# Where the tiles lie in memory, and the order of an opening: a hybrid decoder block on one core

## The chip, the cores and the metric

The kernel runs on one core of a Trainium2 chip. The metric is the device time of one execution in microseconds (us). Three runs of the kernel before took 1753.73, 1755.06 and 1755.92 us; the median, 1755.06, is what the change is compared with.

The engines have short names in the profile. PE is TensorE, which multiplies matrices; PEld is its load of the stationary operand; DVE is VectorE; ACT is ScalarE; POOL is GpSimd; SP issues most DMAs. SBUF is the on-chip memory of 128 partitions. Every tile has an address, the same in each partition, given here in KiB from the low end.

## The reference

x has 256 rows (tokens) and 2048 columns, all in float32. One layer is computed: a SwiGLU feed-forward network (FFN) at half weight, a mixer, and a second FFN.

```python
for l in range(DEPTH):                      # DEPTH = 1
    x = x + 0.5 * swiglu_ffn(rms_norm(x, ffn1_norm[l]), ffn1_w_gate[l], ffn1_w_up[l], ffn1_w_down[l])
    z = rms_norm(x, mix_norm[l]) @ w_in[l]              # 2048 -> 5120, five parts of 1024
    ...                                                 # conv + RG-LRU * gelu, and a gated short conv
    y = jnp.concatenate([rms_norm(y_lru, lru_out_norm[l]), rms_norm(y_sc, sc_out_norm[l])], axis=-1)
    x = x + y @ w_out[l]
    x = x + 0.5 * swiglu_ffn(rms_norm(x, ffn2_norm[l]), ffn2_w_gate[l], ffn2_w_up[l], ffn2_w_down[l])
return rms_norm(x, final_norm)

def rms_norm(x, gain):
    return x * rsqrt(mean(x * x, axis=-1) + 1e-6) * gain

def swiglu_ffn(x, w_gate, w_up, w_down):                # 2048 -> 5632 -> 2048
    return (silu(x @ w_gate) * (x @ w_up)) @ w_down
```

## The kernel before, in words

**Weights in two parts.** A float32 operand is split into a rounded part `hi` and a rest `lo`, and a product is built from hi x hi, lo x hi and hi x lo. Weights come in units of 4 x 128 rows by 512 columns, 1 MB each. `load` (L155) issues a unit's DMA into a raw tile; `parts_of` (L169) makes `hi` by a copy on ScalarE and `lo` by a subtraction on VectorE. TensorE streams `hi` and `lo` as the moving operand, 512 columns wide, and holds a 128 x 128 piece of the activations as the stationary one (`multiply`, L194). One unit is 24 matmuls when it meets both row blocks of x, 12 when it meets one. In the mixer (`columns`) the roles are the other way round.

**Pools and their places.** Pools are declared in this order and lie one above another in that order, from the low end: `const` (with `xres`, the 256 x 2048 x of 16 KiB, to 22 KiB), `raws` (3 raw tiles of 8 KiB, to 46), `splits` (two `hi` from 46 to 62, two `lo` from 62 to 78), `bigs` (ten tiles of 8 KiB for activations in two parts, 78 to 158), `work` (to 163). On top stands the pool of the FFN that is running, `fp` (L406): 13 tiles `keep` of 2 KiB (163 to 189), one more `hi` and one more `lo` (189 to 205), and two raw tiles tagged `kept` (205 to 221). While an FFN runs, every third unit that is split takes the `hi` and `lo` of that pool (L171 to L174); the others take turns at the two of `splits`. In the mixer there is no such pool, and two pools of the mixer's own stand in its place.

**An FFN.** The first 512 columns of gate and up are computed as usual, in eight units named g and u (`ps_g`, `ps_u`). The remaining 5120 columns go in five steps of 1024. Each step treats two row blocks of x by two column blocks of the weight as a 2 x 2 product, done with seven multiplications instead of eight (`seven`, L344). Its operands are sums of blocks: weight sums are made by VectorE in the raw tiles, and the sums of x's blocks once by `seven_of` (L314), whose first call makes `spare` and splits it and whose second part, `rest`, makes three more sums and splits them. In the first FFN these are tiles named `xs`; for the down projection the same is done with the hidden activations in the `keep` tiles, named `hs`. Units named `_p` belong to the seven products (12 matmuls), units named `_x` to the rest of the inner dimension (24).

**The opening of the first FFN.** x is in transposed form only after TensorE's transposes (`Norm.turn`, L220, with four column blocks of 128 per call). The row factor of the norm, 1/sqrt(mean of squares), is not known at first: the first eight units use x times the gain without it, and the factor is put on their results. For the later blocks, `plain` joins x's two parts in float32 (`v`), `normalise` multiplies `v` by the row factor spread over the columns (`norm.bc`, made by `rows` with two small matmuls) and splits it again, and `sums` calls `seven_of`. The squares are sums along rows by ScalarE (`squares`, L213), one instruction for each of four column blocks and two row blocks; `factor` adds them and calls `inv_sqrt` (L257), whose square root is on ScalarE, with a table load ahead of it.

**What sets the order.** Each engine works through its instructions in one order. As long as `Engine.pinned` is true, calls through `pe`, `act` and `dve` stay in program order; that holds from the first unit to the end of the second up unit (L522). Elsewhere a planner may pull an instruction ahead when its operands are ready. DMA issues on SP aren't pinned. The dictionary `follow` (L477) names what is called behind each unit of the opening, and `meanwhile` (L600) what is called within a block: at the first step, `sums` again (which then is `rest`) and `normalise(3)`.

Of the kernel before, what the change touches and what calls it, by code (L numbers as in the profile page):

```python
# [10 lines left out]
F32 = mybir.dt.float32  # L11
F32R = mybir.dt.float32r
AF = mybir.ActivationFunctionType
# [3 lines left out]
P = 128  # L17
D = 2048
# [30 lines left out]
def hybrid_block(ctx: ExitStack, tc: tile.TileContext, a: dict, out: bass.AP):  # L49
# [22 lines left out]
            owed[0] -= cost  # L72

    const = ctx.enter_context(tc.tile_pool(name="const", bufs=1))
    raws = ctx.enter_context(tc.tile_pool(name="raws", bufs=3))
    splits = ctx.enter_context(tc.tile_pool(name="splits", bufs=2))
    bigs = ctx.enter_context(tc.tile_pool(name="bigs", bufs=10))
    work = ctx.enter_context(tc.tile_pool(name="work", bufs=2))
    psum = ctx.enter_context(tc.tile_pool(name="psum", bufs=8, space=bass.MemoryType.PSUM))

    def bank(name):
# [3 lines left out]
        return ap.bitcast(F32)  # L85


    xres = const.tile([P, NT, D], F32, name="xres")

    def load_x(c):  # L90
        cs = slice(c * CW, (c + 1) * CW)
        nc.sync.dma_start(xres[:, :, cs], x[:, cs].rearrange("(t p) d -> p t d", p=P))
# [53 lines left out]
    def big(name):  # L146

        return bigs.tile([P, UK, 2 * S], F32R, tag="big", name=name)
# [6 lines left out]
    def load(src, name, pieces=((0, UK),), loaded=None, kept=False):  # L155
        if kept is None and extra and not turn_of["hold"]:
            turn_of["raw"] += 1
            kept = turn_of["raw"] % 5 > 2
        if kept:
            raw = extra[0].tile([P, UK, CW], F32, tag="kept", name=f"raw_{name}", bufs=2)  # L160
        else:
            raw = raws.tile([P, UK, CW], F32, tag="raw", name=f"raw_{name}")
        for i, e in pieces:
            nc.sync.dma_start(raw[:, i:e, :], src[i * P : e * P].rearrange("(j p) c -> p j c", p=P))
            if loaded:
                loaded(i)
        return raw
# [39 lines left out]
    class Norm:  # L207
# [2 lines left out]
            self.xT = [None] * (KD // UK)  # L210
            self.ss = work.tile([P, NT, NC_D], F32, tag="ss", name=f"ss_{name}")

        def squares(self, c):  # L213
            for t in range(NT):
                junk = work.tile([P, CW], F32, tag="junk", name=f"junk_{self.name}_{c}_{t}", bufs=1)
                act.activation(
                    junk, xres[:, t, c * CW : (c + 1) * CW], AF.Square, accum_out=self.ss[:, t, c : c + 1]
                )

        def turn(self, ks, plain=None):  # L220

# [35 lines left out]
    def inv_sqrt(tot, n, name, w=NT):  # L257
        def t(tag):
            return work.tile([P, w], F32, tag=f"{tag}{w}", name=f"{tag}_{name}")

        v, s, y, q, r = (t(tag) for tag in "vsyqr")
        dve.tensor_scalar(v, tot, 1.0 / n, EPS, op0=ALU.mult, op1=ALU.add)
        act.activation(s, v, AF.Sqrt)
        dve.reciprocal(y, s)
        dve.tensor_tensor(q, y, y, op=ALU.mult)
        dve.tensor_tensor(q, q, v, op=ALU.mult)
        dve.tensor_scalar(q, q, -0.5, 1.5, op0=ALU.mult, op1=ALU.add)
        dve.tensor_tensor(r, y, q, op=ALU.mult)
        return r


# [131 lines left out]
        done(0, 0, d, [s1])  # L403

    def ffn(tag, norm, after, opening=False):
        with tc.tile_pool(name=f"ffn{tag}", bufs=1) as fp:  # L406
            extra.append(fp)
            turn_of["hold"] = True
            wg, wu, wd = (a[f"ffn{tag}_w_{s}"][0] for s in ("gate", "up", "down"))

# [30 lines left out]
            def room(u):  # L441
                for t in range(NT):
                    vs[t, u] = quad(keep(f"v{tag}_{u}_{t}"))
                return {t: vs[t, u] for t in range(NT)}

            def plain(u):

                x = f32(norm.xT[u])
                for t, v in room(u).items():
                    dve.tensor_tensor(  # L450
                        v, x[:, :, t * P : (t + 1) * P], x[:, :, S + t * P : S + (t + 1) * P], op=ALU.add
                    )
# [22 lines left out]

            if opening:
                follow = {  # L477
                    (0, "u"): [lambda: plain(0)],
                    (1, "u"): [flush, lambda: plain(1)],
                    (2, "g"): [norm.rows, lambda: normalise(0)],  # L480
                    (2, "u"): [lambda: normalise(1), sums],
                    (3, "g"): [lambda: normalise(2)],
                }
            else:
                follow = {
                    (0, "g"): [flush],
                    (0, "u"): [norm.factor, lambda: plain(0)],
                    (1, "g"): [norm.rows, lambda: plain(1), lambda: normalise(0)],
                    (1, "u"): [lambda: normalise(1), sums, lambda: plain(2)],
                    (2, "g"): [lambda: normalise(2), lambda: plain(3)],  # L490
                }
            ps = {(m, t): bank(f"ps_{m}{tag}_0_{t}") for m in "gu" for t in range(NT)}
            Engine.pinned = opening
            for u in range(KD // UK):
                for m, w in (("g", wg), ("u", wu)):
                    n = f"{m}{tag}_0_{u}"
                    src = w[u * UK * P : (u + 1) * UK * P, :CW]
                    if opening and (u, m) == (0, "g"):
                        pieces = ((0, 1), (1, 2), (2, 4))
                        raw = load(src, n, pieces, lambda i: load_x(1) if i == 1 else None)  # L500
                        blk = parts_of(raw, n, pieces, lambda i: norm.turn((i,) if i < 2 else (2, 3)))
                        for j in range(UK):
                            for t in range(NT):
                                yh, yl = stationary(norm.xT[u], t)[j]
                                pe.matmul(ps[m, t], yh, blk[j][0], start=j == 0, stop=False)
                                pe.matmul(ps[m, t], yl, blk[j][0], start=False, stop=False)
                                pe.matmul(ps[m, t], yh, blk[j][1], start=False, stop=False)
                        continue
                    raw = load(src, n)
                    if opening and u < 2 and m == "u":  # L510
                        load_x(u + 2)
                    blk = parts_of(raw, n, ((0, 2), (2, 4)), (lambda i: None) if opening else None)
                    if opening and u < 3 and m == ("u" if u < 2 else "g"):
                        if u == 2:
                            norm.squares(3)
                            norm.factor()
                        norm.turn(range(4 * u + 4, 4 * u + 8), room(u + 1) if u else None)
                        for c in ((0, 1), (2,), ())[u]:
                            norm.squares(c)
                    multiply([(ps[m, t], stationary(norm.xT[u], t), u == 0, u == 3) for t in range(NT)], blk)  # L520
                    pump(1.5)
                    if (u, m) == (1, "u"):  # L522
                        Engine.pinned = False
                    for fn in follow.get((u, m), ()):
                        fn()
            units.append(big(f"x{tag}_3"))
            xs = list(enumerate(units))[2:]
            for t in range(NT):
                sg = keep(f"sg{tag}_0_{t}")
# [47 lines left out]
            for s in range(5):  # L577
                cs = (CW + 2 * s * CW, 2 * CW + 2 * s * CW)
                sg = {}

                def total(ps, tiles):
                    for p in tiles[1:]:
                        dve.tensor_tensor(tiles[0], tiles[0], p, op=ALU.add)
                    if not tiles:
                        return ps
                    dve.tensor_tensor(tiles[0], ps, tiles[0], op=ALU.add)
                    return tiles[0]

                def gate(t, n, ps, tiles):
                    g = total(ps, tiles)  # L590
                    sg[t, n] = tiles[0] if tiles else keep(f"z{tag}_{s}")
                    act.activation(sg[t, n], g, AF.Silu)

                def up(t, n, ps, tiles):
                    dve.tensor_tensor(sg[t, n], total(ps, tiles), sg[t, n], op=ALU.mult)
                    if (t, n) == (1, 0):
                        settle()
                    waiting.append((1 + 2 * s + n, t, sg[t, n], s % 2 == 0))

                def meanwhile(i):  # L600
                    if i == 1:
                        settle()
                    elif s == 0:
                        (sums, lambda: normalise(3))[i // 2]()

                seven(wg, (0, 1), cs, sf, xs, f"g{tag}_{s}", keep, gate, meanwhile)
                seven(wu, (0, 1), cs, sf, xs, f"u{tag}_{s}", keep, up)
                if s % 2 == 0:
                    down(s == 4)
# [341 lines left out]
```

## Time and profile before

| What | Value |
|---|---|
| Median of three runs | 1755.06 us |
| Lowest and highest run | 1753.73 and 1755.92 us |
| Span of the profiled execution, from its first to its last instruction | 1753.8 us |
| Busy: PE, DVE, ACT | 1734.0, 1490.1, 1049.6 us |
| Mean granted clock of TensorE | 0.997 |
| DMA, mean over the span | 196 GB/s |

The page gives the span of the profiled execution and no other time of it; the span lies 1.3 us under the median. A page's line of an engine gives its busy time, the share of the span and the number of instructions. In the timeline, a row merges instructions of one kind that follow one another; its first number is the start in us, the second the time from the start of the first to the end of the last. Tile names are without their numbers. L42 is the helper through which all calls of the three engines go, so rows are told apart by tiles.

### The profile page before, as it was taken

What the parts mean: (1) busy time and instruction counts of PE and PEld (TensorE: products, weight loads), DVE (VectorE), ACT (ScalarE), POOL (GpSimd) and SP (SyncE); (2) the same over time, 40 slices, a digit from 0 to 9 for tenths busy, and PEclk for the clock granted to TensorE, in tenths of its full rate; (3) what the DMA queues carried; (4) which work ended last, traced back from release to release, by engine and by line L of the source; (5) the groups of instructions that cost most, each with busy time, mean ns of one, the idle gap of its engine ahead of it and who ended that gap; (6) DMA issues with size and microseconds to landing.
All of it is one profiled execution on the core that took longest, in us unless ns stands there. A gap on an engine that the chain in (4) does not pass through costs nothing. (4 is left out here: it accounts for less than half of the span.)

```text
span 1753.8 us, 20330 instructions
## 1 busy us (share of the span) xinstructions
PE 1734.0 (99%) x8031; PEld 1436.9 (82%) x8031; DVE 1490.1 (85%) x1240; ACT 1049.6 (60%) x1366; POOL 6.9 (0%) x32
## 2 busy tenths in 40 slices
PE   8999999999999999999999999999999999999997
PEld 7788888888888888888888888888788888888886
DVE  6998989889789888587987668989799887899895
ACT  7665565665466666565765455656556654656654
POOL 1000000000000000000000000000000000000000
PEclk9999999999999999999999999999999999999999
DMA  8365655574565555546555763675475546555742
GB/s 313 120 225 181 212 197 192 192 263 173 169 210 190 205 205 188 179 163 207 176 193 169 247 205 130 207 242 180 163 249 199 208 141 228 192 192 192 251 180 98
DMA packets 173904, 343.24 MB, mean 196 GB/s; under 512 B 5620, under 2 KB 8048, under 8 KB 173680
## 3 DMA queue, kind: packets, MB, share of 16 engines
q1 hardware_dynamic: 173344, 340.82, 57.2%
q8 instruction: 63, 1.03, 0.2%
q10 hardware_dynamic: 144, 1.05, 0.2%
q14 instruction: 33, 0.27, 0.0%
q0 software_dynamic: 320, 0.07, 0.0%
HBM read 339.82 MB, written 2.10 MB: 195 GB/s over the span
## 5 line engine op out<-in xcount | busy, mean ns | idle before, releaser
L42 ACT CAST hi_g_p<-raw_g 128x1024 fp32r<-128x1024 f32 x140 | 142.3, 1049 | 111.1 <-DVE raw_g L42 54.4
L42 DVE TENSOR_TENSOR lo_g_p<-raw_g,hi_g_p 128x2048 fp32r<-128x2048 f32 x70 | 159.7, 2287 | 31.8 <-ACT hi_g_p L42 31.7
L42 ACT CAST hi_u_p<-raw_u 128x1024 fp32r<-128x1024 f32 x140 | 141.1, 1049 | 71.1 <-DVE raw_u L42 26.6
L42 DVE TENSOR_TENSOR lo_u_p<-raw_u,hi_u_p 128x2048 fp32r<-128x2048 f32 x70 | 159.2, 2287 | 19.5 <-ACT hi_u_p L42 19.1
L42 PE MATMUL ps_d<-hi_d,h 128*128 128x512 f32 x704 | 169.5, 392 | 0.0
L42 PEld LDWEIGHTS ps_d<-hi_d,h 128*128 128x128 f32 x704 | 131.5, 188 | 28.2
L42 PE MATMUL ps_in<-xT_nm,hi_in 128*128 128x512 f32 x640 | 153.4, 391 | 0.0
L42 PEld LDWEIGHTS ps_in<-xT_nm,hi_in 128*128 128x128 f32 x640 | 117.4, 188 | 23.3 <-ACT tha L42 0.4
L42 ACT CAST hi_d<-raw_d 128x1024 fp32r<-128x1024 f32 x88 | 88.3, 1048 | 69.8 <-PE ps_u_d L42 22.7
L42 DVE TENSOR_TENSOR lo_d<-raw_d,hi_d 128x2048 fp32r<-128x2048 f32 x44 | 100.6, 2291 | 32.8 <-ACT hi_d L42 32.8
L42 DVE TENSOR_TENSOR lo_in<-raw_in,hi_in 128x2048 fp32r<-128x2048 f32 x40 | 91.3, 2284 | 38.9 <-ACT hi_in L42 38.3
L42 ACT CAST hi_in<-raw_in 128x1024 fp32r<-128x1024 f32 x80 | 80.1, 1047 | 67.3 <-PE ps_in L42 45.8
L42 ACT CAST hi_d_p<-raw_d 128x1024 fp32r<-128x1024 f32 x84 | 84.3, 1047 | 52.1 <-DVE raw_d L42 37.8
L42 ACT CAST hi_g_x<-raw_g 128x1024 fp32r<-128x1024 f32 x80 | 81.5, 1050 | 42.1 <-PE ps_g_c L42 26.7
L42 DVE TENSOR_TENSOR lo_d_p<-raw_d,hi_d_p 128x2048 fp32r<-128x2048 f32 x42 | 95.5, 2288 | 13.0 <-ACT hi_d_p L42 12.8
L42 ACT CAST hi_u_x<-raw_u 128x1024 fp32r<-128x1024 f32 x80 | 80.5, 1049 | 37.8 <-PE ps_u_c L42 22.4
L42 DVE TENSOR_TENSOR raw_u<-raw_u,raw_u 128x2048 f32<-128x2048 f32 x40 | 91.5, 2289 | 9.1 <-DMA raw_u<-in_ffn_w_up_dram 8.6
L42 DVE TENSOR_TENSOR raw_g<-raw_g,raw_g 128x2048 f32<-128x2048 f32 x40 | 91.4, 2287 | 7.7 <-DMA raw_g<-in_ffn_w_gate_dram 7.3
L42 DVE TENSOR_TENSOR lo_g_x<-raw_g,hi_g_x 128x2048 fp32r<-128x2048 f32 x40 | 91.4, 2286 | 4.2 <-ACT hi_g_x L42 4.2
L42 DVE TENSOR_TENSOR lo_u_x<-raw_u,hi_u_x 128x2048 fp32r<-128x2048 f32 x40 | 91.4, 2286 | 1.4 <-ACT hi_u_x L42 0.9
L42 PE MATMUL ps_d<-lo_d,h 128*128 128x512 f32 x352 | 87.6, 390 | 0.0
L42 PEld LDWEIGHTS ps_in<-xT_nm,lo_in 128*128 128x128 f32 x640 | 82.1, 191 | 3.1
(347 smaller groups left out, 3597.0 us busy)
## 6 DMA issues: line engine op xcount, KB each, us to landing
raw_u<-in_ffn_w_up_dram SPq DMA_DIRECT2D x88, 1024.0 KB, 5.2
raw_d<-in_ffn_w_down_dram SPq DMA_DIRECT2D x88, 1024.0 KB, 5.2
raw_g<-in_ffn_w_gate_dram SPq DMA_DIRECT2D x87, 1024.0 KB, 5.3
raw_in<-in_w_in_dram SPq DMA_DIRECT2D x40, 1024.0 KB, 5.1
raw_o<-in_w_out_dram SPq DMA_DIRECT2D x16, 1024.0 KB, 5.0
xres<-in_x_dram SPq DMA_DIRECT2D x4, 512.0 KB, 8.1
fin<-in_final_norm_dram ACTq DMA_DIRECT2D x1, 1024.0 KB, 5.8
out_dram<-xres SPq DMA_DIRECT2D x4, 256.0 KB, 2.7
```

The source lines that it names most:

```text
L42: ins = getattr(self.engine, name)(*args, **kwargs)
```

## The change

Three things are changed.

*Places.* `raws` and `work` are declared from the right end of the memory, and so is a new pool `stream` that takes `xres` out of `const`. The `kept` raw tiles move from the FFN's pool into a pool `more` at the right end. From the left now follow `const` (to 6 KiB), `splits` (6 to 38), `bigs` (38 to 118) and the FFN's pool with `keep`, `hi` and `lo` (118 to 160).

*The opening.* Six of the eight squares of the first norm go to VectorE, as a multiplication with a sum along the row. All squares and `factor` now stand behind the transposes of the first up unit; before, the last squares and `factor` stood ahead of those of the third gate unit. The last two quarters of x are loaded behind the first up unit. `rows`, `plain`, `normalise` and `sums` are called one or more units sooner, and both calls of `sums` and `normalise(3)` come before the first block.

*`inv_sqrt`.* Four instructions behind the reciprocal become three.

```diff
     const = ctx.enter_context(tc.tile_pool(name="const", bufs=1))
-    raws = ctx.enter_context(tc.tile_pool(name="raws", bufs=3))
     splits = ctx.enter_context(tc.tile_pool(name="splits", bufs=2))
     bigs = ctx.enter_context(tc.tile_pool(name="bigs", bufs=10))
-    work = ctx.enter_context(tc.tile_pool(name="work", bufs=2))
+    stream = ctx.enter_context(tc.tile_pool(name="stream", bufs=1, side="right"))
+    raws = ctx.enter_context(tc.tile_pool(name="raws", bufs=3, side="right"))
+    work = ctx.enter_context(tc.tile_pool(name="work", bufs=2, side="right"))
...
-    xres = const.tile([P, NT, D], F32, name="xres")
+    xres = stream.tile([P, NT, D], F32, name="xres")
...
-            raw = extra[0].tile([P, UK, CW], F32, tag="kept", name=f"raw_{name}", bufs=2)
+            raw = extra[1].tile([P, UK, CW], F32, tag="kept", name=f"raw_{name}", bufs=2)
...
-        def squares(self, c):
+        def squares(self, c, engine=None):
             for t in range(NT):
...
+                if engine is dve:
+                    junk = work.tile([P, CW], F32, tag="junkv", name=f"junkv_{self.name}_{c}_{t}", bufs=1)
+                    dve.scalar_tensor_tensor(junk, x, 1.0, x, op0=ALU.mult, op1=ALU.mult, accum_out=part)
...
-        dve.tensor_tensor(q, y, y, op=ALU.mult)
+        dve.scalar_tensor_tensor(q, y, -0.5, y, op0=ALU.mult, op1=ALU.mult)
         dve.tensor_tensor(q, q, v, op=ALU.mult)
-        dve.tensor_scalar(q, q, -0.5, 1.5, op0=ALU.mult, op1=ALU.add)
-        dve.tensor_tensor(r, y, q, op=ALU.mult)
+        dve.scalar_tensor_tensor(r, q, 1.5, y, op0=ALU.add, op1=ALU.mult)
...
-        with tc.tile_pool(name=f"ffn{tag}", bufs=1) as fp:
-            extra.append(fp)
+        with (
+            tc.tile_pool(name=f"ffn{tag}", bufs=1) as fp,
+            tc.tile_pool(name=f"more{tag}", bufs=1, side="right") as mp,
+        ):
+            extra.extend((fp, mp))
...
-                    (0, "u"): [lambda: plain(0)],
-                    (1, "u"): [flush, lambda: plain(1)],
-                    (2, "g"): [norm.rows, lambda: normalise(0)],
-                    (2, "u"): [lambda: normalise(1), sums],
-                    (3, "g"): [lambda: normalise(2)],
+                    (1, "g"): [norm.rows, lambda: plain(0)],
+                    (1, "u"): [flush, lambda: normalise(0), lambda: plain(1)],
+                    (2, "g"): [lambda: normalise(1), sums],
+                    (2, "u"): [lambda: normalise(2), sums],
+                    (3, "g"): [lambda: normalise(3)],
...
-                    if opening and u < 2 and m == "u":
-                        load_x(u + 2)
+                    if opening and (u, m) == (0, "u"):
+                        load_x(2)
+                        load_x(3)
+                    if opening and (u, m) == (0, "u"):
+                        norm.squares(0, dve)
                     blk = parts_of(raw, n, ((0, 2), (2, 4)), (lambda i: None) if opening else None)
                     if opening and u < 3 and m == ("u" if u < 2 else "g"):
-                        if u == 2:
-                            norm.squares(3)
+                        norm.turn(range(4 * u + 4, 4 * u + 8), room(u + 1) if u else None)
+                        if u == 0:
+                            norm.squares(1)
+                            norm.squares(2, dve)
+                            norm.squares(3, dve)
                             norm.factor()
-                        norm.turn(range(4 * u + 4, 4 * u + 8), room(u + 1) if u else None)
-                        for c in ((0, 1), (2,), ())[u]:
-                            norm.squares(c)
...
-                    elif s == 0:
+                    elif s == 0 and not opening:
                         (sums, lambda: normalise(3))[i // 2]()
```

More of the change, by code (lines that the diff above doesn't have):

```diff
@@ L211, in __init__ @@
             self.ss = work.tile([P, NT, NC_D], F32, tag="ss", name=f"ss_{name}")
-        def squares(self, c):
+        def squares(self, c, engine=None):
             for t in range(NT):
[L215 to L218, printed above, removed]
+                x, part = xres[:, t, c * CW : (c + 1) * CW], self.ss[:, t, c : c + 1]
+                if engine is dve:
+                    junk = work.tile([P, CW], F32, tag="junkv", name=f"junkv_{self.name}_{c}_{t}", bufs=1)
+                    dve.scalar_tensor_tensor(junk, x, 1.0, x, op0=ALU.mult, op1=ALU.mult, accum_out=part)
+                else:
+                    junk = work.tile([P, CW], F32, tag="junk", name=f"junk_{self.name}_{c}_{t}", bufs=1)
+                    act.activation(junk, x, AF.Square, accum_out=part)
         def turn(self, ks, plain=None):
@@ L525, in ffn @@
                         fn()
-            units.append(big(f"x{tag}_3"))
+            if not opening:
+                units.append(big(f"x{tag}_3"))
             xs = list(enumerate(units))[2:]
```

## The prediction, made before the change was run

> **What bounds the kernel now.** The page comes first, for the bounding engine.
>
> ```profile
> span 1753.8 us, 20330 instructions
> PE 1734.0 (99%) x8031; PEld 1436.9 (82%) x8031; DVE 1490.1 (85%) x1240; ACT 1049.6 (60%) x1366; POOL 6.9 (0%) x32
> ```
>
> TensorE (PE) is busy for 99% of the span. Only two things can give time: PE's few waits, and the pace of its matmuls. So the timeline of PE comes next, in a stretch without waits. Columns: start, time of the group, engine, line, operation, out<-in.
>
> ```profile
> 526.47 1.98 PE L42 MATMUL ps_u_a<-hi_u_p,xs 128*128 128x512 f32 x8
> ...
> 529.19 2.01 PE L42 MATMUL ps_u_c<-hi_u_p,xs 128*128 128x512 f32 x8
> ...
> 531.96 2.01 PE L42 MATMUL ps_u_d<-hi_u_x,x 128*128 128x512 f32 x8
> ...
> 537.45 1.98 PE L42 MATMUL ps_u_a<-hi_u_p,x 128*128 128x512 f32 x8
> ...
> 540.17 2.01 PE L42 MATMUL ps_u_a<-hi_u_x,x 128*128 128x512 f32 x8
> ...
> 545.68 1.03 PE L42 MATMUL ph<-ident,u_g 128*128 128x128 f32 x8
> ```
>
> The matmuls are pipelined, so the pace is the distance from one unit's first start to the next one's. The units here take 2.72 us for 12 matmuls (from 526.47 and from 537.45, 227 ns each), 2.77 for 12 (from 529.19), 5.49 for 24 (from 531.96) and 5.51 for 24 (from 540.17); at the first pace 24 would take 5.44. The slow and fast ones follow a period of three: fast, slow by 0.05 to 0.07, slow by 0.05. The code has one thing of that period: line 173 puts every third split unit's hi and lo into the FFN's own pool (call these X), the next into the first buffer of `splits` (A), the next into its second (B). Counting the units in the order of the calls, the one from 529.19 is X, from 531.96 A, from 537.45 B, from 540.17 X. By the order and the sizes of the pools X lies at 189 to 205 KiB of each partition, A and B at 46 to 78, the stationary tiles of `bigs` at 78 to 158. So a matmul that streams from the high end is slow, and so is the A unit behind it; a B unit, whose two operands and predecessor are low, is not. The other operand can be tried too: the `hs` tiles lie in the FFN's pool (163 to 189 KiB) and are stationary.
>
> ```profile
> 182.16 1.09 PE L42 MATMUL ps_d_a<-lo_d_p,hs 128*128 128x512 f32 x4
> 183.09 0.85 PE L42 MATMUL ps_d_c<-hi_d_p,hs 128*128 128x512 f32 x3
> ```
>
> Four matmuls in 0.93 us, 232 ns each, are the slowest steady pace of the two views. Then the waits of PE (engine and tile, what it waited for, total, times, longest):
>
> ```profile
> PE ps_g_c L42 <- DVE x L42: 2.3, 1, 2.3
> PE ps_g_e L42 <- ACT hi_g_x L42: 0.8, 1, 0.8
> PE ps_g_c L42 <- ACT hi_g_p L42: 0.7, 1, 0.7
> ```
>
> These three, 3.8 us, lie in the first 2x2 block of the first FFN, between 59 and 74 us. Last the stretches around them (busy of PE, PEld, DVE, ACT, POOL, granted clock, DMA share, GB/s):
>
> ```profile
> 10.00:15.00 5.00, 4.49 (x20) 3.23 (x19) 2.37 (x3) 3.04 (x3) 0.00 (x0) 1.00 1.05 389
> 15.00:20.00 5.00, 5.00 (x28) 4.28 (x27) 4.07 (x8) 4.52 (x13) 0.00 (x0) 1.00 1.05 387
> 20.00:25.00 5.00, 5.00 (x24) 4.09 (x23) 4.20 (x4) 4.84 (x6) 0.00 (x0) 1.00 1.05 386
> 25.00:30.00 5.00, 5.00 (x28) 4.22 (x27) 4.72 (x7) 3.55 (x11) 0.00 (x0) 1.00 1.04 381
> 30.00:35.00 5.00, 5.00 (x28) 4.23 (x27) 3.21 (x4) 5.00 (x13) 0.00 (x0) 1.00 1.04 385
> 35.00:40.00 5.00, 5.00 (x25) 3.96 (x24) 3.08 (x13) 4.97 (x15) 0.00 (x0) 1.00 0.90 325
> ...
> 70.00:75.00 5.00, 2.73 (x11) 1.87 (x11) 5.00 (x5) 2.46 (x4) 0.00 (x0) 0.95 0.55 199
> 75.00:80.00 5.00, 5.00 (x18) 3.95 (x17) 5.00 (x4) 1.86 (x3) 0.00 (x0) 0.71 0.59 170
> ```
>
> VectorE is full from 70 to 80 us while PE waits; behind the longest wait the clock is 0.95 and 0.71, which costs 5 x (0.05 + 0.29) = 1.7 us. From 10 to 40 us VectorE is idle for 30 - 21.65 = 8.35 us.
>
> **The change, part by part.** *Memory.* Declared from the left now lie small constants, `splits`, `bigs` and the FFN's pool, which end at 160 KiB; `xres`, `raws`, `work` and the kept raw tiles lie at the right end. X, `hs` and the FFN's other tiles come below 160 KiB, where bigs run at B's pace up to 158. Splits move to 6 to 38 KiB, which no row shows for a 512-wide operand; I take them as low. The number of split units is read from VectorE's groups:
>
> ```profile
> L42 DVE TENSOR_TENSOR lo_g_p<-raw_g,hi_g_p 128x2048 fp32r<-128x2048 f32 x70 | 159.7, 2287 | 31.8 <-ACT hi_g_p L42 31.7
> L42 DVE TENSOR_TENSOR lo_u_p<-raw_u,hi_u_p 128x2048 fp32r<-128x2048 f32 x70 | 159.2, 2287 | 19.5 <-ACT hi_u_p L42 19.1
> L42 DVE TENSOR_TENSOR lo_d<-raw_d,hi_d 128x2048 fp32r<-128x2048 f32 x44 | 100.6, 2291 | 32.8 <-ACT hi_d L42 32.8
> L42 DVE TENSOR_TENSOR lo_d_p<-raw_d,hi_d_p 128x2048 fp32r<-128x2048 f32 x42 | 95.5, 2288 | 13.0 <-ACT hi_d_p L42 12.8
> ...
> L42 DVE TENSOR_TENSOR lo_u_x<-raw_u,hi_u_x 128x2048 fp32r<-128x2048 f32 x40 | 91.4, 2286 | 1.4 <-ACT hi_u_x L42 0.9
> L42 DVE TENSOR_TENSOR lo_g_x<-raw_g,hi_g_x 128x2048 fp32r<-128x2048 f32 x40 | 91.4, 2286 | 4.2 <-ACT hi_g_x L42 4.2
> ...
> L42 DVE TENSOR_TENSOR lo_d_x<-raw_d,hi_d_x 128x2048 fp32r<-128x2048 f32 x20 | 45.7, 2284 | 0.0
> ```
>
> 326, and the 16 units of the two openings make 342, so 114 triples. X: 0.05 where the unit has 12 matmuls (182 of the 342), 0.07 where it has 24 (160), 0.059 in the mean, 6.7 us. A: 114 x 0.05 = 5.7 us. `hs` serves four of the seven products in each of six blocks, 24 x 12 matmuls x (232 - 227) ns = 1.4 us. Together 13.8 us, of which I take nine tenths, 12.5, since the differences of 0.05 are read to 0.01. Against it: the transposes read `xres`, which goes from the low end to the high one. At the price of one A unit, 0.05, for each of their 12 groups (four in each of three norms) this is 0.6 us. Between 0 and 13.8 I keep -12.0. VectorE's and ScalarE's reads of raw tiles cost nothing extra: some of the raw tiles in the groups above lie above 205 KiB today, the others below 46, and the means are within 7 ns.
>
> The Trainium skill (SBUF — State Buffer, section "Who interferes with whom") says that TensorE and ScalarE never wait on anyone at their memory ports and gives no dependence on the address. By it the layout is worth 0 and the sum below is 12.0 us smaller; the pace of 227 against 232 ns above speaks against leaving address out, and the rule about others' accesses isn't tested by it.
>
> *Opening.* The prices:
>
> ```profile
> 16.82 0.65 ACT L42 ACTIVATE junk_n<-xres 128x512 f32<-128x512 f32 x1
> 17.34 0.22 ACT L42 ACTIVATION_READ_ACCUMULATOR junk_n<-xres 128x1 f32 x1
> ...
> 19.73 1.98 ACT L42 CAST hi_g<-raw_g 128x1024 fp32r<-128x1024 f32 x2
> ...
> 21.30 3.84 PE L42 MATMUL ps_g<-hi_g,xT_n 128*128 128x512 f32 x16
> ...
> 36.08 1.28 ACT L42 ACT_TABLE_LOAD   x1
> ...
> 37.38 0.20 ACT L42 ACTIVATE s_n<-v_n 128x2 f32<-128x2 f32 x1
> ...
> 60.22 0.68 DVE L42 TENSOR_TENSOR v<-v,v 128x512 f32<-128x512 f32 x1
> ```
>
> Six of eight squares leave ScalarE (about 0.76 each by start to start, 4.5 us) for VectorE. No row shows a square there; the nearest, 0.68 for two inputs of that size, gives 4.1 us, and with an accumulator read like ScalarE's 0.22 it would be 5.4. I take 4.1. Squares 0 stand ahead of lo_u, while VectorE waits for hi_u: hidden. Squares 2 and 3, the sum and the square root now stand ahead of the second gate unit's hi_g. ScalarE has two squares less but the table load more there: 16.82 + 2 x 0.76 + 1.28 = 19.6, then it waits for VectorE, which finishes four lo of xT at 17.9 and four squares by 20.4, and sum and mean by 20.7. Square root, then hi_g from 20.9 instead of 19.73; its first half, 1.0 us, ends at 21.9 and PE wanted it at 21.30. hi_u and what follows on ScalarE stand behind. Loss 0.6; with the accumulator reads 1.4; I take +0.9.
>
> The four norm operations become three; two instructions on 128x2 fewer in the path are under 0.4 us and inside that number. The row factor's matmuls follow the second gate unit on PE's fixed order: they start no sooner than 21.3 + 0.9 + 24 x 0.227 = 27.6. VectorE's copy of bc waits for them, with plain(0) and the next lo_u behind it; VectorE may stand idle from its lo_g's end near 24.5 to 27.6. lo_u is wanted 16 matmuls later, near 32; it needs about 0.4 + 1.4 + 1.2 after 27.9, so PE doesn't wait for its first half.
>
> The DMA of x's last quarter goes ahead of the second gate unit on SP's queue: 0.5 MB at 387 GB/s, 1.4 us later for that unit, which ScalarE now wants only at 20.9. POOL's queue isn't passed. No cost; without that cover at most 1.4.
>
> What it buys: sums and normalise(3) leave the first block, where VectorE is full. Since all of that work stays on VectorE, PE gets back only what moves into the idle 8.35 us: less 4.1 for squares, and less 0 to 3.1 for the wait on bc and 0.35 for the square root. That is 0.8 to 4.0 us; I take 2.8, near the upper end, since plain(1) and the next units' lo, which aren't in fixed order, can fill the wait. With less waiting, half of the clock's 1.7 comes too: -3.6, between 0 and 5.5 (3.8 + 1.7). Late next is lo of the last opening units and the first p4 of the block, which follow the same full VectorE.
>
> Sum: -12.0 + 0.9 - 3.6, and +0.4 back: the gain in pace, 12.0 of some 1700 us or 0.7%, is worth nothing in the first 55 us of the blocks, where VectorE stays full. That is -14.3: span 1739.5 after 1753.8. The median of the three runs, 1755.06, is 1.3 above that span; -14.3 from it is 1740.8.
>
> **The rivals.** *The address does nothing.* The period of three would belong to the single buffer of X or to the waits that come with it, not to its place. For it: A is slow too, and its place is low. Against: `hs` is in no such buffer. Only the opening's -2.7 is left: 1752.4. This is also where the Trainium skill's rule of the SBUF page would lead.
>
> *Only the pace goes, not the tails.* A's 5.7 us may follow from the change of pool. Then 1746.5.
>
> *VectorE fills sooner.* If idle time isn't used, the stalls move ahead of the block instead of going: 0 for the 3.6, and 3 us more at the last lo of the opening (VectorE then stands a unit late, 2.29 from the groups, and 0.68 for one square). 1755.06 - 12.0 + 0.9 + 0.4 + 3 = 1747.4.
>
> *The low end becomes the crowded one (slower).* What slows X may be the traffic of the FFN's pool on the same stretch of memory, where VectorE and ScalarE read and write all the time, and not the distance. Then `splits`, `bigs` and that pool, now neighbours, all run at X's pace. 114 B units and the mixer's and output's 56 at 0.06 give +10 us: 1755.06 + 10 - 2.7 = 1762.4. It decides from 45 units on, where 0.06 each passes the opening's 2.7. For it: nothing tells the two apart by address alone. Against: A and B stand beside `raws`, which VectorE and ScalarE read and DMA fills just as often, and B is fast.
>
> **How the numbers follow.** My forecast 0.55 (1740.8; its own range 1735.8, with 13.8 and 5.5 in full, to 1745). VectorE fills sooner 0.15. Address does nothing 0.13. Tails stay 0.07. Crowded 0.10. The range 1735.8 to 1753 leaves out the crowded case and a little of the forecast's edges; without 1752.4 more than 2 in 10 would be out. Within 0.2% is 3.5 us, about what a measurement of this kernel can tell from no change. Faster: 0.55 + 0.15 + 0.07 and a quarter of 0.13, 0.80. Same: the rest of that case, 0.10. Slower: 0.10.
>
> **What would show it.** Right: every split unit of the FFNs, whichever its place in three, at 2.72 us for 12 and 5.44 for 24; `hs` units at 227 ns; no wait of ps_g_c for x; the clock 1.00 at 70 to 80 us; one wait of PE of about 0.9 us near 21 us for hi_g. Wrong: the period of three stays; the second gate unit waits over 1.5 us; waits for lo_u or lo_g between 40 and 60 us; the mixer's units slow down.

## The result, and the profile after

The changed kernel took 1749.76 us (median of six runs, 1748.43 to 1750.99), the kernel before, run beside it, 1755.05 (1753.73 to 1756.61). The ratio is 0.9968, with a 95% interval of 0.9957 to 0.9979. It is 5.3 us faster, where 14.3 were forecast; the time lies inside the range, between the rivals "VectorE fills sooner" (1747.4) and "The address does nothing" (1752.4).

The page of the changed kernel, for its bounding engine:

```profile
span 1748.6 us, 20335 instructions
PE 1724.4 (99%) x8031; PEld 1436.9 (82%) x8031; DVE 1491.9 (85%) x1247; ACT 1045.3 (60%) x1354; POOL 6.9 (0%) x32
```

PE is busy 9.6 us less with the same 8031 instructions, but the span is only 5.2 us shorter. So the matmuls became faster and the waits longer. First the matmuls: PE's timeline for the two stretches that were shown of before, the units with `hs` and then the same five kinds of unit in the same order.

```profile
183.97 1.98 PE L42 MATMUL ps_d_a<-hi_d_p,hs 128*128 128x512 f32 x8
185.78 1.07 PE L42 MATMUL ps_d_a<-lo_d_p,hs 128*128 128x512 f32 x4
186.69 0.84 PE L42 MATMUL ps_d_c<-hi_d_p,hs 128*128 128x512 f32 x3
...
527.02 1.98 PE L42 MATMUL ps_u_a<-hi_u_p,xs 128*128 128x512 f32 x8
...
529.74 1.98 PE L42 MATMUL ps_u_c<-hi_u_p,xs 128*128 128x512 f32 x8
...
532.46 1.98 PE L42 MATMUL ps_u_d<-hi_u_x,x 128*128 128x512 f32 x8
...
537.90 1.98 PE L42 MATMUL ps_u_a<-hi_u_p,x 128*128 128x512 f32 x8
...
540.62 1.98 PE L42 MATMUL ps_u_a<-hi_u_x,x 128*128 128x512 f32 x8
```

Start to start the units from 527.02 on take 2.72, 2.72, 5.44 (24 matmuls) and 2.72 us, where before had 2.72, 2.77, 5.49 and 2.72. The period of three is gone, also where `hs` is stationary, in the three rows ahead. Eight of these take 1.81 us and four 0.91, 226 to 228 ns each. Then the waits of PE (engine and tile, what it waited for, total, times, longest):

```profile
PE ps_g_c L42 <- ACT hi_g_p L42: 3.5, 1, 3.5
...
PE ps_g_a L42 <- DVE lo_g_p L42: 1.6, 1, 1.6
PE ps_d_a L42 <- DVE lo_d_p L42: 1.2, 3, 0.9
PE ps_u L42 <- DVE lo_u L42: 1.2, 2, 0.7
PE ps_g L42 <- ACT hi_g L42: 0.8, 1, 0.8
```

The wait of `ps_g_c` for `x` (2.3 us) and that of `ps_g_e` (0.8) are gone. In their place stand 3.5 us for `hi_g_p` (0.7 before), 1.6, 1.2 for `lo_u` and 0.8; the row of `lo_d_p` belongs to the down projection, at 181 us and later. Three stretches of VectorE's, ScalarE's and PE's timelines show how these come about; the number in brackets is the idle time ahead of the row and what ended it.

```profile
18.32 0.68 DVE L42 SCALAR_TENSOR_TENSOR junkv_n<-xres 128x512 f32<-128x512 f32 x1
18.93 0.08 DVE L42 DVE_READ_ACCUMULATOR junkv_n<-xres 128x1 f32 x1
19.05 0.69 DVE L42 SCALAR_TENSOR_TENSOR junkv_n<-xres 128x512 f32<-128x512 f32 x1
...
21.71 0.20 ACT L42 ACTIVATE s_n<-v_n 128x2 f32<-128x2 f32 x1 [1.48 <-DVE v_n L42]
21.82 1.98 ACT L42 CAST hi_g<-raw_g 128x1024 fp32r<-128x1024 f32 x2
...
22.91 2.38 PE L42 MATMUL ps_g<-hi_g,xT_n 128*128 128x512 f32 x9 [0.82 <-ACT hi_g L42]
...
25.16 0.47 DVE L42 TENSOR_SCALAR diag_n<-ident,r_n 128x128 f32<-128x128 f32 x2
29.18 0.42 DVE L42 COPY bc_n<-pb_n 128x256 f32<-128x256 f32 x1 [3.54 <-PE pb_n L42]
29.52 1.28 DVE L42 TENSOR_TENSOR v<-xT_n 128x512 f32<-128x512 f32 x2
30.72 2.35 DVE L42 TENSOR_TENSOR lo_u<-raw_u,hi_u 128x1024 fp32r<-128x1024 f32 x2
...
38.17 2.35 DVE L42 TENSOR_TENSOR lo_g<-raw_g,hi_g 128x1024 fp32r<-128x1024 f32 x2
...
59.00 1.20 PE L42 MATMUL ps_u<-lo_u,xT_n 128*128 128x512 f32 x4 [0.68 <-DVE lo_u L42]
...
63.41 1.41 DVE L42 SCALAR_TENSOR_TENSOR sg<-ps_u,r_n,sg 128x512 f32<-128x512 f32 x2
...
64.72 4.61 DVE L42 TENSOR_TENSOR raw_g<-raw_g,raw_g 128x2048 f32<-128x2048 f32 x2
...
67.10 1.99 ACT L42 CAST hi_g_p<-raw_g 128x1024 fp32r<-128x1024 f32 x2 [1.73 <-DVE raw_g L42]
...
68.20 3.35 PE L42 MATMUL ps_g_c<-hi_g_p,xs 128*128 128x512 f32 x7 [3.45 <-ACT hi_g_p L42]
```

And the windows around them (busy of PE, PEld, DVE, ACT, POOL, granted clock, DMA share, GB/s):

```profile
25.00:30.00 5.00, 5.00 (x30) 4.26 (x29) 1.46 (x5) 3.20 (x5) 0.00 (x0) 1.00 1.06 387
...
60.00:65.00 5.00, 2.60 (x9) 1.35 (x8) 5.00 (x6) 1.24 (x3) 0.00 (x0) 1.00 0.82 280
65.00:70.00 5.00, 1.80 (x4) 1.49 (x5) 4.97 (x3) 3.27 (x5) 0.00 (x0) 0.53 0.02 7
70.00:75.00 5.00, 5.00 (x19) 3.85 (x18) 5.00 (x3) 3.58 (x5) 0.00 (x0) 0.79 0.02 3
```

VectorE stands idle for 3.54 us in front of the copy of `bc`, which waits for the two small matmuls behind the second gate unit. From 25 to 30 us it is busy 1.46 us (4.72 before). That idle time is missed 30 us later: `lo_u` comes late, then `lo_g_p`, then the first weight difference (`raw_g`), and with it ScalarE's `hi_g_p` and PE at 68.20.

To see where the 5.3 us come from, take the distance from each matmul's start to the next one's in both traces, and split it at 23 ns above the usual distance of a matmul of that width: what lies below is pace, a distance beyond it is a stall, which then counts in full. A matmul at half clock, some 427 ns in place of 227, counts as a stall too. The sums, in us over the whole trace:

| Part | Before | After | Difference |
|---|---|---|---|
| Pace, against 226.7 ns for 512 columns | 11.1 | -1.1 | -12.2 |
| Stalls up to 14 us | 5.9 | 6.7 | +0.8 |
| Stalls from 14 to 90 us | 6.9 | 10.8 | +3.9 |
| Stalls after 90 us | 5.8 | 8.3 | +2.5 |
| First matmul to last | 1742.0 | 1736.9 | -5.1 |

The pace came as forecast. The opening, which was to bring 2.7 us, took 3.9 in its own stretch.

### The profile page after: what moved, and what is told of

It reads as the page before. It is cut to its first block, busy times and chain, and to the rows that moved or that the text cites. A ratio compares the mean times of both kernels' runs of the same rounds, so it can differ in the third digit from the quotient of the medians.

```text
span 1748.6 us, 20335 instructions
## 1 busy us (share of the span) xinstructions
PE 1724.4 (99%) x8031; PEld 1436.9 (82%) x8031; DVE 1491.9 (85%) x1247; ACT 1045.3 (60%) x1354; POOL 6.9 (0%) x32
## 5 line engine op out<-in xcount | busy, mean ns | idle before, releaser
L42 ACT CAST hi_u_x<-raw_u 128x1024 fp32r<-128x1024 f32 x80 | 80.5, 1047 | 33.3 <-PE ps_u_c L42 20.7
```

Of the source, the lines that this page charges most:

```text
L42: ins = getattr(self.engine, name)(*args, **kwargs)
```

## The experiments

Theory at the start (the prediction's, with the result): memory brings about 11 us because the high addresses are gone; the opening loses some 5 because VectorE idles at `bc`. Rivals: the layout works through something other than the height of the address; the opening's loss belongs to other steps.

### The two parts alone

`layout` is the kernel before with only the new places; `opening` is the changed kernel with the old ones. The diff is the core of `layout` against the kernel before; `xres`, the `kept` tiles and the pool `more` go with it, and in `opening` the same lines are turned back.

```diff
-    raws = ctx.enter_context(tc.tile_pool(name="raws", bufs=3))
-    work = ctx.enter_context(tc.tile_pool(name="work", bufs=2))
+    stream = ctx.enter_context(tc.tile_pool(name="stream", bufs=1, side="right"))
+    raws = ctx.enter_context(tc.tile_pool(name="raws", bufs=3, side="right"))
+    work = ctx.enter_context(tc.tile_pool(name="work", bufs=2, side="right"))
...
```

> The kernel before with the new places of the tiles alone; opening and norm as before. Theory 1 (the two parts add, the opening is a loss of its own): the pace of the 512-wide matmuls gives 12 us, of which 0.5 to 2.5 come back where VectorE is full, so 1743 to 1746 us, 3 to 6 us under the changed kernel. Rival (a faster TensorE meets the full VectorE anyway, the opening is neutral): about 1750, as the changed kernel.

> The changed kernel with the tiles at their old places, so the new opening and norm alone. Theory 1: the new opening loses 4 to 5 us by itself: 1759 to 1760, the waits of the first block near 10 us instead of 6. Rival (opening neutral alone): 1754 to 1756.

`layout` took 1744.98 us (1743.79 to 1745.80), ratio 0.9939 [0.9924, 0.9953]. `opening` took 1759.91 (1759.04 to 1762.30), ratio 1.0027 [1.0017, 1.0036]. Against 1755.84 for the kernel before, run beside them, these are -10.9 and +4.1, which add to -6.8 where the whole change gave -5.3. The opening is a loss by itself. Its waits are those of the whole change, 3.5, 1.6, 1.2 and 0.8 us, and the stalls of its stretch from 14 to 90 us are 10.8 us again.

### The wait on bc

`late_bc` is the changed kernel with one instruction moved: VectorE's copy of `bc` out of PSUM stands behind `lo` of the second up unit and the transposed parts of x that follow it.

```diff
         def rows(self, split=False):
...
+            self.pb = pb
+            if not split:
+                self.spread()
+
+        def spread(self):
             self.bc = work.tile([P, S], F32, tag="bc", name=f"bc_{self.name}")
-            dve.tensor_copy(self.bc, pb[:, :S])
+            dve.tensor_copy(self.bc, self.pb[:, :S])
...
-                    (1, "g"): [norm.rows, lambda: plain(0)],
+                    (1, "g"): [lambda: norm.rows(True), lambda: plain(0)],
...
                         norm.turn(range(4 * u + 4, 4 * u + 8), room(u + 1) if u else None)
...
+                        if u == 1:
+                            norm.spread()
```

> The changed kernel, but VectorE's copy of bc stands behind the lo and the xT of the second up unit instead of ahead of plain(0). In the changed kernel VectorE stood 3.5 us idle at that copy. If this wait is what the opening loses: VectorE idle near 0 from 25 to 29 us, the waits of PE in the first block smaller by about 3.5 us and the slow clock with them, 1744 to 1746. If the opening loses by the order of sums and normalise ahead of the last units: less than 1.5 us better, 1748 to 1750.

It took 1745.55 us (1743.12 to 1747.18), ratio 0.9941 [0.9926, 0.9956]: 4.2 less than the changed kernel. VectorE's timeline in it:

```profile
24.78 0.48 DVE L42 TENSOR_SCALAR diag_n<-ident,r_n 128x128 f32<-128x128 f32 x2
25.17 1.29 DVE L42 TENSOR_TENSOR v<-xT_n 128x512 f32<-128x512 f32 x2
26.38 2.35 DVE L42 TENSOR_TENSOR lo_u<-raw_u,hi_u 128x1024 fp32r<-128x1024 f32 x2
28.65 1.22 DVE L42 TENSOR_TENSOR lo_g<-raw_g,hi_g 128x1024 fp32r<-128x1024 f32 x1
...
33.94 0.41 DVE L42 COPY bc_n<-pb_n 128x256 f32<-128x256 f32 x1
```

and its waits:

```profile
PE ps_g_c L42 <- ACT hi_g_p L42: 3.1, 1, 3.1
PE ps_d_a L42 <- DVE lo_d_p L42: 1.1, 2, 0.9
PE ps_g L42 <- ACT hi_g L42: 0.9, 1, 0.9
```

The gap is filled with the same work that had stood behind the copy. `lo_u` starts at 26.38 and not at 30.72, `lo_g` of the third gate unit at 28.65 and not at 38.17. The waits for `lo_u` and for `lo_g_p` of 1.6 us are gone from PE's list, and the stalls from 14 to 90 us fall from 10.8 to 6.2 us. Not all of it is waits: behind its 3.1 us wait this trace keeps the full clock, which is worth 1.8 of these 4.6 us, and it is the fastest of four runs of which two took 1746.91 and 1747.18. Still, the copy is all that was moved, and by the medians it returns 4.2 us where `opening` lost 4.1. So the wait on `bc` is what the opening lost, with the slow clock that followed. One wait stays, 3.1 us for `hi_g_p`, and it is why the opening still gains nothing over `layout`.

### High, or only near

`mirror` is `layout` turned over: the tiles that TensorE reads (`splits`, `bigs`, the FFN's pool) at the high end, from 70 to 224 KiB, and the raw weights, `xres` and `work` at the low end. `raws`, `work` and the two pools of an FFN are turned over as the lines here are.

```diff
-    splits = ctx.enter_context(tc.tile_pool(name="splits", bufs=2))
-    bigs = ctx.enter_context(tc.tile_pool(name="bigs", bufs=10))
-    stream = ctx.enter_context(tc.tile_pool(name="stream", bufs=1, side="right"))
+    splits = ctx.enter_context(tc.tile_pool(name="splits", bufs=2, side="right"))
+    bigs = ctx.enter_context(tc.tile_pool(name="bigs", bufs=10, side="right"))
+    stream = ctx.enter_context(tc.tile_pool(name="stream", bufs=1))
...
```

> The kernel before with raw tiles, x and small tiles at the low end and TensorE's tiles at the high end, in the order FFN pool (70 to 112 KiB), bigs (112 to 192), splits (192 to 224). No raw tile is a neighbour above 70 KiB. Theory address (an operand above some 160 KiB is slow, whatever lies beside it): units of splits, two of three, at 2.76 us and more for 12, units of the FFN's pool at 2.72 only behind such a unit's tail; bigs slow from the 7th tile on; sum 15 to 30 us over the layout at the low end, 1758 to 1775. Rival neighbours (slow is what shares a stretch with raw tiles that DMA and VectorE write): every unit at 2.72, 1743 to 1746.

It took 1745.35 us (1744.78 to 1745.99), ratio 0.9941 [0.9927, 0.9956], as fast as `layout`. PE's timeline, the same kinds of unit:

```profile
522.62 1.98 PE L42 MATMUL ps_u_a<-hi_u_p,xs 128*128 128x512 f32 x8
...
525.33 1.98 PE L42 MATMUL ps_u_c<-hi_u_p,xs 128*128 128x512 f32 x8
...
528.05 1.98 PE L42 MATMUL ps_u_d<-hi_u_x,x 128*128 128x512 f32 x8
...
533.49 1.98 PE L42 MATMUL ps_u_a<-hi_u_p,x 128*128 128x512 f32 x8
```

2.71, 2.72 and 5.44 us, with `splits` at 192 to 224 KiB, where X had lain before, and higher. **The height of the address costs nothing; the prediction's cause is false.**

### The low bits of the address

What else did the layout change? In the kernel before, `work` stands between `bigs` and the FFN's pool. Its tiles add up to 5952 bytes per partition, which is 23 x 256 + 64. `splits` and `bigs` are made of tiles of 8 KiB, so all of those start at the same place modulo 2048, and everything in the FFN's pool (X, `hs`) is out of step with them. In `layout` and in `mirror` `work` is on the other side and nothing of an odd size stands between the pools that TensorE reads. The new theory: the addresses of TensorE's two operands have to agree in their low bits. The test is an unused tile, written once at the start and never read:

```diff
+    gap = ctx.enter_context(tc.tile_pool(name="gap", bufs=1))
+    nc.gpsimd.memset(gap.tile([P, N // 4], F32, name="gap"), 0.0)
     psum = ctx.enter_context(tc.tile_pool(name="psum", bufs=8, space=bass.MemoryType.PSUM))
```

`before_pad192` puts 192 bytes behind `work` in the kernel before (5952 + 192 = 24 x 256). The others put N bytes behind `bigs` in `layout`, which is in step without them.

> The kernel before with one unused tile of 192 bytes per partition between work and the FFN's pool; nothing else moves. In the kernel before, all tiles of splits and bigs start at 1568 modulo 2048 bytes, those of the FFN's pool at 1376, since work isn't a whole number of 2 KiB; with the 192 bytes all start at 1568. Theory alignment (TensorE is slow when its operands' addresses differ in their low bits, and for some ten matmuls after a change): the period of three goes, all split units at 2.72 us for 12, 1743 to 1746 us. Rival neighbours (X and hs are slow because raw tiles that DMA fills lie beside them at the high end, or between the tiles of TensorE): nothing changes, 1755.

> The new places alone (1745.0), with one unused tile of 64 bytes between bigs and the FFN's pool. Alignment: the FFN's pool is off by 64 bytes, as it is modulo 128 in the kernel before (192 bytes), so the period of three comes back and 12 us with it: 1755 to 1758. Neighbours: nothing changes, 1745.

> As layout_pad64 with 128 bytes. Alignment within 128 bytes: fast, 1745. Alignment within 256 bytes or more: slow, 1750 to 1758. Neighbours: 1745.

> As layout_pad64 with 1024 bytes. Alignment within 1024 bytes or less: fast, 1745. Within 2048 or more: slow, 1750 to 1758. Neighbours: 1745.

> The memory part alone with an unused 256-byte tile between bigs and the FFN's pool. With 64 and 128 bytes there it was 1755.9 and 1758.3, with 1024 it was 1746.4, with none 1745.0. If the addresses of TensorE's two operands have to agree only in the bits below 256, it is 1744 to 1747. If they have to agree modulo 512 or 1024, it is 1754 to 1759, with the split units of the FFN's pool at 229 ns for a 512-wide matmul again.

> The same with 512 bytes. If the modulus is 256 or 512, 1744 to 1747. If it is 1024, 1754 to 1759.

The offset in the table is that of the FFN's pool against `bigs`, modulo 256; the pace is the mean distance of 512-wide matmuls, over the distances under 250 ns.

| Run | Offset | Median, us | Ratio to before, 95% interval | Pace, ns |
|---|---|---|---|---|
| before | 64 | 1755.05 | | 228.81 |
| `before_pad192` | 0 | 1746.09 | 0.9949 [0.9934, 0.9964] | 227.05 |
| `layout` | 0 | 1744.98 | 0.9939 [0.9924, 0.9953] | 227.04 |
| `layout_pad64` | 64 | 1755.85 | 1.0002 [0.9993, 1.0012] | 228.79 |
| `layout_pad128` | 128 | 1758.31 | 1.0017 [1.0007, 1.0027] | 229.17 |
| `layout_pad256` | 0 | 1745.58 | 0.9942 [0.9925, 0.9959] | 227.08 |
| `layout_pad512` | 0 | 1745.52 | 0.9941 [0.9926, 0.9956] | 227.04 |
| `layout_pad1024` | 0 | 1746.36 | 0.9949 [0.9933, 0.9965] | 227.05 |
| `mirror` | 0 | 1745.35 | 0.9941 [0.9927, 0.9956] | 227.13 |

PE's timeline of `layout_pad64`:

```profile
527.57 1.98 PE L42 MATMUL ps_u_a<-hi_u_p,xs 128*128 128x512 f32 x8
...
530.29 2.01 PE L42 MATMUL ps_u_c<-hi_u_p,xs 128*128 128x512 f32 x8
...
533.05 2.01 PE L42 MATMUL ps_u_d<-hi_u_x,x 128*128 128x512 f32 x8
...
538.54 1.98 PE L42 MATMUL ps_u_a<-hi_u_p,x 128*128 128x512 f32 x8
```

2.72, 2.76 and 5.49 us: 64 bytes bring back the period of three and the whole time of the kernel before, with every split weight and every stationary tile below 161 KiB. And 192 bytes take it out of the kernel before with X as high as it was. Offsets of 256, 512 and 1024 are as good as none, 64 and 128 are not, so here the step is 256 bytes. It is the offset between the pools that counts and not the place of either: the tiles start at 32 modulo 256 in `layout` and at 224 in `mirror`, and both are fast.

The single distances from matmul to matmul in the kernel before show which part of a unit is slow. In the A unit from 531.96 us (the second kind, moving tile from `splits`, behind a unit of X) only the first ten are uneven, 223 to 236 ns; the other fourteen are 225 to 228. In the X unit from 540.17 us they stay uneven to the end, 225 to 236. A moving tile of X with a stationary `hs` of the same pool is a pair in step. By the count of split units the first two rows here are such a unit, and the third begins one of `hs` with a tile of `splits`:

```profile
422.13 2.01 PE L42 MATMUL ps_d_a<-hi_d_p,hs 128*128 128x512 f32 x8
423.98 1.08 PE L42 MATMUL ps_d_a<-lo_d_p,hs 128*128 128x512 f32 x4
424.90 2.03 PE L42 MATMUL ps_d_c<-hi_d_p,hs 128*128 128x512 f32 x8
```

Its first ten distances are 224 to 236 ns, the last two 226 and 227; from 424.90 us on all eight are 233 or 234. So a pair out of step is slow for as long as it lasts, and a change from one place to another costs a tail of some ten matmuls, even where the new pair is in step. Such a tail also stands behind a wait: in `layout`, from 176.65 us, nine distances of 224 to 236 ns and then 226, behind a wait of 0.90 us.

What stays open is what in the chip does this. An offset was tried only between whole pools, and none but 64, 128 and multiples of 256 bytes.

### What remains of the opening

`late_bc` still waits 3.1 us for `hi_g_p` of the first weight difference. Two runs move work on VectorE from in front of that difference to behind it: `late_sg` the two products `sg`, `late_sg_x` also `normalise(3)`. Both start from `late_bc`; `gated` is the product that `hold` puts off, and the two lines on `normalise(3)` are in `late_sg_x` alone.

```diff
                 act.activation(sg, ps["g", t], AF.Silu, scale=norm.r[:, t : t + 1])
-                dve.scalar_tensor_tensor(sg, ps["u", t], norm.r[:, t : t + 1], sg, op0=ALU.mult, op1=ALU.mult)
+                if opening:
+                    hold.append((t, sg))
...
-                    (3, "g"): [lambda: normalise(3)],
...
+                    elif s == 0 and opening and i == 0:
+                        for t, v in hold:
+                            gated(t, v)
+                        normalise(3)
```

> The changed kernel with VectorE's copy of bc behind the second up unit's lo (1745.6), and in addition the two products of the first gate and up column (sg, 1.41 us of VectorE) moved behind the first weight difference of the first 2x2 block. If VectorE's order ahead of that difference sets TensorE's wait of 3.05 us near 62 us there, the wait falls by about 1.4 and the time is 1743.5 to 1745. If the wait only moves to the next lo on VectorE, it stays at 1745 to 1746.5.

> As the one before, and normalise(3) moved there too (another 2.8 us of VectorE). If the wait is set by what stands ahead of the difference, nothing is left of it and the time is 1742 to 1744. If VectorE is short of time over the whole first block, the 2.8 us come back as a wait for x near 70 us (2.3 us in the kernel before) and the time is 1745 to 1747.

`late_sg` took 1745.90 us (1743.91 to 1746.72), no better than `late_bc`. Its wait in the first block:

```profile
PE ps_g_c L42 <- ACT hi_g_p L42: 2.4, 1, 2.4
```

and the window behind the wait:

```profile
65.00:70.00 5.00, 5.00 (x19) 3.95 (x18) 5.00 (x3) 2.97 (x4) 0.00 (x0) 0.67 0.00 0
```

The wait shrank by 0.7 us, but here the clock falls behind it, and eight matmuls of some 427 ns cost 1.6 us, which the trace of `late_bc` doesn't have. With four runs of each, spread over 2.8 and 4.1 us, a gain of 0.7 can't be told from none. `late_sg_x` took 1742.43 us (1741.46 to 1743.56), ratio 0.9923 [0.9909, 0.9938], the shortest of all kernels here. In its list of waits no row of the first block is over 0.3 us; the timeline shows why:

```profile
58.02 2.29 DVE L42 TENSOR_TENSOR raw_g<-raw_g,raw_g 128x2048 f32<-128x2048 f32 x1
60.22 1.41 DVE L42 SCALAR_TENSOR_TENSOR sg<-ps_u,r_n,sg 128x512 f32<-128x512 f32 x2
...
61.50 2.12 PE L42 MATMUL ps_g_c<-hi_g_p,xs 128*128 128x512 f32 x8
```

The first difference starts at 58.02, where the changed kernel had two of them together from 64.72, and PE goes on at 61.50 without a wait. Its stalls from 14 to 90 us are 4.1 us, 2.9 less than in the kernel before, 1.6 of it by the clock. The median is 13.4 us below that of the kernel before, run beside it (1755.81).

## Why the prediction was wrong, step by step

**Memory, -12.0: right in size, wrong in cause.** The pace gave -12.2 us, and alone the layout gave -10.9. The sum of X, A and `hs` (13.8, less a tenth) held because it was read from rows of pace and not from the cause. The transposes of `xres`, costed at 0.6, show no loss: the pace from 14 to 90 us went from +0.2 to -0.1 us. That the new places took the loss away was luck: `layout_pad64` has places as low and gains nothing (1755.85). The cause, "a matmul that streams from the high end is slow", fails in `mirror` and `before_pad192`. The prediction had noted that X and `hs` share a pool, and took from it the pool's height; that this pool sits behind one of an odd size could be read from the same list. Its own remark that nothing tells two causes apart "by address alone" was a reason to ask which property of the address it is. The Trainium skill (SBUF — State Buffer, section "Who interferes with whom") would have given the layout nothing; the measured 10.9 us decides against leaving the address out. The Trainium skill (SBUF — State Buffer, section "Operand start alignment") asks only that an operand start at a multiple of its element size and says of its runs that they timed nothing; all nine kernels of the table keep that rule and differ by up to 13.3 us.

**hi_g late, +0.9: right in size.** PE waited 0.82 us. The square root came at 21.71 and not near 20.7: the squares began at 18.32 and not at 17.9, and took 0.73 each start to start where 0.68 was taken. PE itself came about 0.8 us later to this point, through the stalls of the first 14 us; `late_sg_x`, with the same code there, has 5.8 us of them, as the kernel before has, so that they are not the change's. The forecast wait came out because `hi_g` and PE both came 0.8 to 0.9 us later than forecast, which is luck.

**The wait on bc: the step that failed.** The prediction saw the idle time ("from its lo_g's end near 24.5 to 27.6") and wrote that "plain(1) and the next units' lo, which aren't in fixed order, can fill the wait". In the trace nothing fills it: 3.54 us, and no instruction from behind the copy ran ahead of it. The part ahead of the prediction says itself that calls keep their order to the end of the second up unit. The copy, `plain(0)` and that unit's `lo_u` stand in that stretch, and work that is free to move stayed behind them all. With the copy alone moved, 4.2 us come back by the medians. It was also right that PE doesn't wait for `lo_u` near 32 us; the debt shows at 59 us and later, since VectorE has no slack in between.

**Sums out of the block, -3.6: not there.** The wait for `x` is gone as forecast, but waits of 1.2, 1.6 and 3.45 us stand ahead of it, so that the stretch lost 3.9 us. The clock, of which half the 1.7 us was to come back, gave nothing: it is 0.53 and 0.79 from 65 to 75 us. Counted as the prediction does, that is 5 x (0.47 + 0.21) = 3.4 us, but PE waited until 68.20, and low clock costs nothing while PE waits. By their distances the matmuls lost 1.8 us to it here and 1.6 in the kernel before. (Two slips in the prediction's sums change nothing here: 8.35 - 4.1 - 0.35 is 3.9 and not 4.0, and the lower bound of 1735.8 leaves out the +0.9 and +0.4.) That the sum was within reach is shown by `late_sg_x`: with VectorE's gap filled and `normalise(3)` and the two `sg` in the block, the opening is worth 2.6 us over `layout` by the medians (1744.98 to 1742.43; the runs don't overlap, the intervals do) and 1.8 by the stalls of its stretch (5.9 to 4.1), near the 2.7 forecast. The better order keeps the sums early and `normalise(3)` late.

**Give-back, +0.4: too small in this trace.** The stalls after 90 us rose by 2.5 us. In `layout` they rose by 1.6, in `late_sg_x` by 1.0, in `late_bc` by 0.4 and in `layout_pad1024` by 2.8, so that single traces scatter too much to size it. A faster TensorE may meet more places where VectorE is full, such as the 0.9 us at `lo_d_p` (0.6 before).

**The rivals.** "VectorE fills sooner" named the right place and nearly the right size: 3 us more at the last `lo` of the opening, against 1.2 + 1.6 measured. It had the first block's waits merely move and not grow, which leaves it 2.4 us below the measured time. "Address does nothing" is wrong, since `layout` alone brings 10.9 us, but right in one point: not the height. "Crowded" and "tails stay" are out: all units run at one pace.

**The signs named ahead.** As forecast: 2.72 and 5.44 for the units shown, `hs` at 227, no wait for `x`, a wait of about 0.9 for `hi_g`. Against it: the clock at 70 to 80 us, and waits for `lo_u`, which were to be a sign of being wrong, ahead of 59.00 and 60.74 us.

## What to carry to other kernels

Look at where the tiles that one engine reads together start, modulo a few hundred bytes, before anything is concluded from how far apart they lie; one pool of an odd size in front of others can cost thousands of matmuls some nanoseconds each, and here a pad of 192 bytes was the whole cure. Before counting on idle time being filled, list what stands behind the waiting instruction in the fixed order: a copy that waits holds all of it. An engine that is nearly full behind an idle stretch pays for it later: here the waits show 30 us behind the place that caused them.

## What was not expected of the hardware

The pace of float32 matmuls with 512 columns depends on the operands' addresses modulo 256: 227.0 ns in the mean with the pools in step, 228.8 with 64 bytes between them and 229.2 with 128, over some 7000 matmuls 12 to 15 us. A pair out of step is slow throughout; a pair in step is uneven only for some ten matmuls behind a change of pools or a wait. Units with `hs` stationary and a moving tile from `splits` went from 232 ns to 227. A wait of PE of 3.45 us in the changed kernel was followed by a granted clock of 0.53 and 0.79 in the next two windows of 5 us; behind one of 3.1 us in `late_bc` it stayed at 1.00, so that waits of nearly the same length cost different amounts. The wait of 2.3 us for `x` near 73 us was followed by 0.71 in the kernel before and by 1.00 in `layout`. A pair of traces can differ by 1.6 us through this alone.
